# A hybrid attention and state-space layer: a third staging tile for weights, spaced norm tasks, deferred decay sums and early output tiles

## The chip, the cores and the metric

The kernel runs on one core of a Trainium2 chip. The metric is the device time of one execution in microseconds, as a median of runs. Smaller is better.

## What is computed

One layer on 2048 tokens of width 1024, in float32. With `hn` the RMSNorm of the tokens `h`, the reference does, cut short:

```python
proj = hn @ w_in[layer]
q, k, v, g_attn, z, xbc, dt_raw, q_mem, g_mem = jnp.split(proj, splits, axis=-1)
att = window_attention(rotary(q), rotary(k), v, attn_sink[layer]) * jax.nn.silu(g_attn)   # window of 128 to both sides
xs, bm, cm = jnp.split(jax.nn.silu(centred_depthwise_conv(xbc, conv_w[layer], conv_b[layer])), ...)
dt = jax.nn.softplus(dt_raw + dt_bias[layer])
y = ssd_scan(xs, dt[:, :, 0], a[0], bm, cm) + ssd_scan(backward) + d_skip[layer] * xs     # chunks of 128 tokens
ssd = gated_group_rmsnorm(y, z, ssd_norm_w[layer])
xat = softmax(q_mem . mk) @ mv * jax.nn.silu(g_mem)                                       # 256 memory tokens
h = h + jnp.concatenate([att, ssd, xat], axis=-1) @ w_out[layer]
return rms_norm(h, norm_out_w)
```

Attention has 16 query heads on 4 key heads of 64, the scan 8 heads of 64 in 2 groups with a state of 128, the memory attention 4 heads of 128.

## The kernel before

Large products are made exact enough by splitting each float32 operand into a rounded high part and a low part (`split`, L193 to L196: a cast on ScalarE, a difference on VectorE) and adding three matmuls (`split3`, L183). `mm` (L171) issues every matmul and `tr` (L179) every transpose, so nearly all of TensorE's work bears the lines L177 and L181.

The tokens go in four chunks of 512, the last first (loop near the end of `layer`, c = 3 to 0). A chunk's normalised and split tokens (xh, xl, 8 tiles each) stay in memory; the weights are streamed. `load_w` (L198) loads 128x1024 weights into a staging tile ws (two of them), and splits them into wh and wl (three each). Per chunk come the keys (`keys`, with the rotation `rope`), the values and step sizes (`values`, `steps`), and then four rounds g: query heads (`heads`), convolution (`conv`), gates (`z_gate`) and memory projection (`mem_project`). Attention, memory attention and the scan inside blocks of 128 tokens run as tasks between these products: `attention`, `mem_attention`, `ssd_local`. `ssd_local` needs for each block and group the decay sums that `ssd_load` (L600) makes from a loaded tile fb: four additions on ScalarE (L610), four on VectorE (L611) and an exponential (L612).

The next chunk's norms are made on the way. `cols_x` and `rstd_cols` (L294 to L306) run at once before round 1: for each of 4 or 5 blocks of tokens two half rows of x are loaded into a tile cu (three) and squared on ScalarE with a sum (L302). `rows_x` spreads the results over the partitions, and `norm_x` (L342) runs at once in round 2: eight tiles of x in transposed form are loaded into xp (four), multiplied on VectorE (L349) and stored. At the chunk's end `prep_x` loads them again into xp and splits them into xh and xl. The first keys' rotation borrows xp tiles as well.

After the last chunk the pools of the projections (`xhl`, `misc`) are closed and the output product begins. `mixed` (L983) loads and splits the mixed rows of a block of 128 tokens (mxl, mxh), `load_wo` (L965) the output weights through ws and xr tiles, `early` (L1004) adds the attention and memory half of a block, `out_block` (L1023) the rest and the final norm. The forward scan across blocks runs as tasks meanwhile: `incoming` (L743) makes what the states bring into a block, `carry` (L589) takes the state on, and `forward` (L774) adds it, gates it, sums squares (L790, L792) and normalises, one block at a time.

What sets the order: TensorE's order is written out by the program. A planner clock, `clock[0]`, is moved by `mm` and `tr` with a fixed cost for each; a task gives way with `yield t` and is taken up again when the planner's clock has gone on by t us (`tick`). `slot` and `reads` do the same for banks of the accumulator memory. `limits` says how many tasks of a kind run at once. The order on the other engines, and of the DMAs on SyncE's queue, is laid by the framework's scheduler at compile time, by a simulated timeline and by priorities (`tc.high_priority` moves instructions ahead), and each engine then runs its own list in that order. `tc.keep_in_program_order` puts an instruction behind the one written before it for the same engine.

## Time and profile before

| | |
|---|---|
| median of three runs | 1847.41 us (1845.33 to 1850.26) |
| the profiled execution | 1848.8 us |
| its span, first to last instruction | 1847.1 us |
| TensorE busy | 1755.7 us, 95% of the span |
| VectorE, ScalarE, GpSimd busy | 1179.9, 921.4, 260.3 us |
| mean granted TensorE clock | 0.985 of full speed |
| DMA | 347.59 MB, 188 GB/s in the mean |

The span is divided among chunks c = 3 to 0 up to about 1390 us, the change to the output product, and the output product with the forward scan from about 1495 to the end. A wait of TensorE stands in a row of the timeline in square brackets, with the instruction that ended it.

### The profile page before, as it was taken

What the parts mean: (1) busy time and instruction counts of PE and PEld (TensorE: products, weight loads), DVE (VectorE), ACT (ScalarE), POOL (GpSimd) and SP (SyncE); (2) the same over time, 40 slices, a digit from 0 to 9 for tenths busy, and PEclk for the clock granted to TensorE, in tenths of its full rate; (3) what the DMA queues carried; (4) which work ended last, traced back from release to release, by engine and by line L of the source; (5) the groups of instructions that cost most, each with busy time, mean ns of one, the idle gap of its engine ahead of it and who ended that gap; (6) DMA issues with size and microseconds to landing.
All of it is one profiled execution on the core that took longest, in us unless ns stands there. A gap on an engine that the chain in (4) does not pass through costs nothing. (4 is left out here: it accounts for less than half of the span.)

```text
span 1847.1 us, 26627 instructions
## 1 busy us (share of the span) xinstructions
PE 1755.7 (95%) x9242; PEld 1426.0 (77%) x9242; DVE 1179.9 (64%) x2681; ACT 921.4 (50%) x1985; POOL 260.3 (14%) x253
## 2 busy tenths in 40 slices
PE   7889999999799999999999989999998999999998
PEld 6878878877578787777778877778776777787886
DVE  7466666688576667778666777977677543443443
ACT  6237645664665566657555654656566411111121
POOL 1000000012200000121000002210111133333321
PEclk9989999999899999999999989999998999999999
DMA  7666364578653854776475466673658586566553
GB/s 237 211 197 187 123 214 146 152 241 244 210 169 122 268 165 150 240 245 206 142 211 161 133 205 195 190 214 118 197 179 265 165 251 182 164 180 180 171 176 120
DMA packets 264422, 347.59 MB, mean 188 GB/s; under 512 B 29536, under 2 KB 172000, under 8 KB 264288
## 3 DMA queue, kind: packets, MB, share of 16 engines
q1 hardware_dynamic: 264288, 345.90, 61.1%
q8 instruction: 73, 1.20, 0.3%
q14 instruction: 61, 0.50, 0.1%
HBM read 254.34 MB, written 91.49 MB: 187 GB/s over the span
## 5 line engine op out<-in xcount | busy, mean ns | idle before, releaser
L177 PE MATMUL pj<-xh,wh 128*128 128x512 f32 (+2 forms) x1296 | 506.6, 391 | 2.8 <-ACT xh L195 1.0
L177 PE MATMUL pj<-xl,wh 128*128 128x512 f32 (+2 forms) x1296 | 494.0, 381 | 4.8 <-DVE xl L196 4.8
L177 PE MATMUL pj<-xh,wl 128*128 128x512 f32 (+2 forms) x1296 | 494.7, 382 | 0.9 <-DVE wl L196 0.8
L196 DVE TENSOR_TENSOR wl<-ws,wh 128x1024 fp32r<-128x1024 f32 (+2 forms) x175 | 212.3, 1214 | 117.3 <-ACT wh L195 112.9
L177 PEld LDWEIGHTS pj<-xh,wl 128*128 128x128 f32 x1296 | 246.0, 190 | 46.9 <-DVE wl L196 2.7
L177 PEld LDWEIGHTS pj<-xh,wh 128*128 128x128 f32 x1296 | 246.7, 190 | 41.9 <-issue 3.7
L177 PEld LDWEIGHTS pj<-xl,wh 128*128 128x128 f32 x1296 | 246.8, 190 | 40.7 <-DVE xl L196 5.9
L195 ACT CAST wh<-ws 128x1024 fp32r<-128x1024 f32 (+2 forms) x175 | 180.0, 1029 | 179.3 <-PE pj L177 127.6
L546 DVE CUSTOM_DVE_ANT_0 pm<-s,band,sink 128x384 f32<-128x384 f32 (+1 forms) x256 | 150.3, 595 | 48.3 <-PE s L177 46.4
L554 ACT ACTIVATE pm<-pm,mx 128x385 f32<-128x385 f32 (+1 forms) x256 | 151.2, 595 | 55.5 <-DVE mx L552 55.5
L177 PE MATMUL pj<-woh,mxh 128*128 128x512 f32 x416 | 169.1, 407 | 0.0
L177 PE MATMUL pj<-woh,mxl 128*128 128x512 f32 x416 | 164.2, 395 | 0.0
L177 PE MATMUL pj<-wol,mxh 128*128 128x512 f32 x416 | 164.1, 394 | 0.0
L648 POOL TENSOR_TENSOR b<-nat,win 128x256 f32<-128x256 f32 x64 | 43.3, 697 | 841.2 <-ACT nat L632 841.2
L558 ACT ACTIVATE pm<-pm,den 128x384 f32<-128x384 f32 (+1 forms) x256 | 133.5, 595 | 6.9 <-DVE den L556 6.8
L572 ACT COPY pt<-t 128x512 f32<-128x512 f32 x120 | 69.4, 583 | 103.6 <-PE t L181 103.3
L195 ACT CAST mxh<-mxl 128x512 fp32r<-128x512 f32 x64 | 39.5, 617 | 162.8 <-DMA mxl<-mix_d 105.7
L181 PE MATMUL t<-ident,pm 128*128 128x128 f32 x736 | 103.8, 276 | 11.6 <-ACT nat L632 6.7
L181 PEld LDWEIGHTS t<-ident,pm 128*128 128x128 f32 x736 | 86.5, 142 | 34.6 <-ACT nat L632 7.6
L177 PE MATMUL s<-khh,qs 128*128 128x384 f32 (+1 forms) x256 | 94.7, 370 | 18.3 <-DVE mx L546 13.8
L484 DVE SCALAR_TENSOR_TENSOR cu<-raw,cw,cu 128x512 f32<-128x512 f32 (+2 forms) x128 | 99.3, 776 | 3.3 <-ACT cu L482 2.0
L177 PE MATMUL o<-pt,vg 128*64 128x256 f32 x736 | 93.8, 388 | 1.6 <-DVE dq L425 0.7
(222 smaller groups left out, 2842.8 us busy)
## 6 DMA issues: line engine op xcount, KB each, us to landing
ws<-in_w_in_dram SPq DMA_DIRECT2D x152, 512.0 KB, 4.2
q_d<-rt SPq DMA_DIRECT2D x32, 512.0 KB, 4.3
qs<-q_d SPq DMA_DIRECT2D x32, 512.0 KB, 6.1
fb<-f_d SPq DMA_DIRECT2D x32, 512.0 KB, 4.4
mxl<-mix_d SPq DMA_DIRECT2D x64, 256.0 KB, 4.1
mix_d<-ao SPq DMA_DIRECT2D x64, 128.0 KB, 3.5
xc<-xbc_d SPq DMA_DIRECT2D x32, 256.0 KB, 3.7
st_d<-carry SPq DMA_DIRECT2D x32, 256.0 KB, 3.9
```

What stands on the lines that cost most here:

```text
L177: nc.tensor.matmul(out, lhsT=lhsT, rhs=rhs, start=start, stop=stop)
L181: nc.tensor.transpose(out, in_, ident)
L195: nc.scalar.copy(hi, x)
L196: (eng or nc.vector).tensor_tensor(lo, x, as32(hi), ALU.subtract)
L484: nc.vector.scalar_tensor_tensor(u, raw[:, r0 + k:r0 + k + cnt], cw[:, i, k:k + 1], u, ALU.mult, ALU.add)
L546: nc.vector.tensor_tensor_reduce(pm[:, r, :w], ss[:, :w], band[:, ms], 1.0, sink8[:, 4 * g + r:4 * g + r + 1], ALU.add, ALU.max, mx[:, r:r ...
L554: nc.scalar.activation(pm[:, r, :w + 1], pm[:, r, :w + 1], AF.Exp, bias=mx[:, r:r + 1], scale=0.125, accum_out=den[:, r:r + 1])
L558: nc.scalar.activation(pm[:, r, :w], pm[:, r, :w], AF.Copy, scale=den[:, r:r + 1])
L572: nc.scalar.copy(pts[j], tt)
L648: nc.gpsimd.tensor_tensor(xd[:, d], nat[:, 0:256].rearrange("p (r e) -> p r e", r=4), win[:, d, 4 * g:4 * g + 4].unsqueeze(2).broadcast_to ...
```

## The change

- `load_w`'s staging tile ws gets three buffers; xp goes from four to three, and dt, fc, win from three to two.
- The squares for the next chunk's norms become a task of the new kind io, started at round 0: three loads go out, 8 us of planner time pass, then one square each 3 us, each followed by the next load. Their tiles are xp in place of cu. The squares are kept in program order. `diag_x` in round 2 waits for the task.
- `norm_x` becomes such a task, started in round 2; its multiplications are kept in program order and spaced by 2 us (5 more before the fourth and the seventh). `prep_x` waits for it.
- `ssd_load` gives back the loaded tile alone. A new `ssd_decay` makes the decay sums. For the first block and group it comes after the 12 us of planner time instead of before, and its first two instructions are kept in program order.
- `mem_attention` gives way for 4.5 instead of 3.0 us before its last product, `incoming` for 8.5 instead of 7.0, `forward` for 13 instead of 11.
- Two `forward` tasks run at once (yy in xc tiles, zz in b0 or b1 by turns), and all of them wait for `ssd_local`. The additions of `incoming` and the addition and gating of `forward` go from GpSimd to VectorE, and so do the state's two operations in `carry` for the forward direction.
- Before the projection pools are closed, block 15's first two mixed tiles are loaded and split in two ws tiles; `early` uses them for its first block. The planner then idles for 3 us. Of the next output weights rows 3 and 15 go through xr and row 13 through the tile nwo, instead of ws. `early` goes on until the third forward block is done instead of the second.

```diff
-    limits = {"att": 3, "mem": 1, "ssd": 1, "inc": 1, "fwd": 1}
+    limits = {"att": 3, "mem": 1, "ssd": 1, "inc": 1, "fwd": 2, "io": 1}
...
+    pin = tc.keep_in_program_order
...
-            ws = wsp.tile([P, D], F32, name="ws", bufs=2)
+            ws = wsp.tile([P, D], F32, name="ws", bufs=3)
...
-    def rstd_cols(src, nblk):
+    def cols_x(c, out):
...
+        def load():
+            if len(tiles) < len(jobs):
+                b, j = jobs[len(tiles)]
+                xn = misc.tile([P, XW], F32, name="xp", bufs=3)[:, :CH]
+                nc.sync.dma_start(xn, a["x"][s + b * P:s + (b + 1) * P, j * CH:(j + 1) * CH])
+                tiles.append(xn)
+
+        for _ in range(3):
+            load()
+        yield 8.0
+        for i, (b, j) in enumerate(jobs):
+            pin(nc.scalar.activation(tiles[i], tiles[i], AF.Square, accum_out=s2[:, j, b:b + 1]))
+            load()
+            yield 3.0
...
-    def norm_x(c, rb):
+    def norm_x(c, out):
...
+        for _ in range(3):
+            load()
+        yield 8.0
+        while "rows" not in out:
+            yield 1.0
         for kt in range(KT):
-            x32 = misc.tile([P, XW], F32, name="xp", bufs=4)[:, :w]
-            nc.sync.dma_start(x32, a["xT"][kt * P:(kt + 1) * P, s:s + w])
-            nc.vector.scalar_tensor_tensor(x32, x32, nw[:, kt:kt + 1], rb[:, :w], ALU.mult, ALU.mult)
-            nc.sync.dma_start(xn_d[kt, :, s:s + w], x32)
+            if kt in (3, 6):
+                yield 5.0
+            pin(nc.vector.scalar_tensor_tensor(tiles[kt], tiles[kt], nw[:, kt:kt + 1], out["rows"][:, :w],
+                                               ALU.mult, ALU.mult))
+            nc.sync.dma_start(xn_d[kt, :, s:s + w], tiles[kt])
+            load()
+            yield 2.0
...
+        eng = nc.gpsimd if d else nc.vector
+        eng.tensor_tensor(new.rearrange("p (r e) -> p r e", r=8), st.rearrange("p (r e) -> p r e", r=8), dec, ALU.mult)
+        eng.tensor_tensor(new, new, s, ALU.add)
...
+        return xc, fb
+
+    def ssd_decay(c, g, fb, first=False):
+        dt, fc, win = dts[c]
         ee = sp.tile([P, 4, P], F32, name="b0")
...
+            if r == 0 and first:
+                pin(i1)
+                pin(i2)
         nc.scalar.activation(ee, ee, AF.Exp)
...
-        nxt = ssd_load(*parts[0])
+        xc, fb = ssd_load(*parts[0])
         yield 12.0
+        nxt = xc, ssd_decay(*parts[0], fb, True)
...
-        nc.gpsimd.tensor_tensor(ef[:, 0], ef[:, 0], ef[:, 1], ALU.add)
+        nc.vector.tensor_tensor(ef[:, 0], ef[:, 0], ef[:, 1], ALU.add)
...
-        yy = sp.tile([P, 4, P], F32, name="b0")
+        yy = sp.tile([P, 4, P], F32, name="xc", bufs=2)
...
-        zz = sp.tile([P, 4, P], F32, name="b1")
+        zz = sp.tile([P, 4, P], F32, name=f"b{c % 2}")
...
-        nc.gpsimd.tensor_tensor(yy, yy, inc[c][:, 0], ALU.add)
+        nc.vector.tensor_tensor(yy, yy, inc[c][:, 0], ALU.add)
...
-            if c and g == 1:
-                cols = cols_x(c - 1)
+            if c and g == 0:
+                ahead = {}
+                cols_t = spawn("io", cols_x(c - 1, ahead))
             if c and g == 2:
-                dg = diag_x(c - 1, cols)
+                need(cols_t)
+                dg = diag_x(c - 1, ahead["cols"])
+                norm_t = spawn("io", norm_x(c - 1, ahead))
...
+    def mixed_tiles(c, qs, los, his):
+        mh, ml = {}, {}
+        for q, lo, hi in zip(qs, los, his):
+            nc.sync.dma_start(as32(lo), mix_d[4 * q:4 * q + 4, :, c * P:(c + 1) * P].rearrange("j p t -> p j t"))
+            split(hi, lo, as32(lo))
+            for j in range(4):
+                mh[4 * q + j], ml[4 * q + j] = hi[:, j], lo[:, j]
+        return mh, ml
+
+    first = [wsp.tile([P, D], F32R, name="ws", bufs=3).rearrange("p (u j t) -> p u j t", u=2, j=4) for _ in range(2)]
+    first = mixed_tiles(NB - 1, (0, 3), *([t[:, 0], t[:, 1]] for t in first))
     wx.close()
     fp = pool("fp")
     wo = pool("wo")
+    idle(clock[0] + 3.0)
...
-        ws = wsp.tile([P, D], F32, name="ws", bufs=2) if k % 2 else fp.tile([P, D], F32, name="xr", bufs=2)
+        ws = (wsp.tile([P, D], F32, name="ws", bufs=3) if k % 2 and pl is not wo else
+              fp.tile([P, D], F32, name="nwo") if k == 13 else fp.tile([P, D], F32, name="xr", bufs=2))
...
-        mh, ml = mixed(c, (0, 3))
+        mh, ml = mixed(c, (0, 3)) if begun else first
...
-    while last > 3 and not fwd[1].done:
+    while last > 3 and not fwd[2].done:
```

## Rows read from the trace of the kernel before

**Rows 1.** The page: the span, and busy time, share and count by engine

```profile
span 1847.1 us, 26627 instructions
PE 1755.7 (95%) x9242; PEld 1426.0 (77%) x9242; DVE 1179.9 (64%) x2681; ACT 921.4 (50%) x1985; POOL 260.3 (14%) x253
```

**Rows 2.** TensorE's timeline: start, length, instruction, [idle before and what ended it]

```profile
70.77 0.39 PE L177 MATMUL pj<-wl,xh 128*128 128x272 f32 x1 [3.06 <-DVE wl L196]
...
128.17 0.69 PE L177 MATMUL s<-khh,qs 128*128 128x384 f32 x1 [6.76 <-DVE mx L546]
...
469.11 0.69 PE L177 MATMUL s<-khh,qs 128*128 128x384 f32 x1 [3.82 <-ACT carry L670]
...
492.64 0.33 PE L181 MATMUL t<-ident,pm 128*128 128x128 f32 x1 [1.12 <-ACT pm L558]
...
499.15 0.48 PE L181 MATMUL t<-ident,pm 128*128 128x128 f32 x1 [4.72 <-ACT nat L632]
...
1095.31 0.49 PE L177 MATMUL o<-pt,mvt 128*128 128x512 f32 x1 [2.06 <-ACT pt L727]
...
1097.68 0.80 PE L177 MATMUL o<-mpm,mvt 128*128 128x512 f32 x1 [1.88 <-DVE mpm L731]
...
1403.38 0.79 PE L177 MATMUL pj<-wh,mxh 128*128 128x512 f32 x1 [8.86 <-ACT mxh L195]
```

**Rows 3.** Windows: stretch, length, PE busy (count), granted clock, DMA share, GB/s

```profile
123.80:134.04 10.24, 5.87 (x15) 0.50 0.36 100
468.55:471.96 3.41, 2.85 (x8) 0.50 0.63 207
495.86:502.68 6.82, 3.53 (x11) 0.50 0.56 162
...
1096.60:1103.43 6.83, 5.75 (x16) 0.50 0.89 265
1396.97:1407.21 10.24, 3.83 (x9) 0.50 1.00 336
```

**Rows 4.** ScalarE's timeline, the first decay sums

```profile
122.73 1.28 ACT L610 ACTIVATE b<-fb,fc 128x128 f32<-128x128 f32 x4 [6.24 <-DMA fb<-f_d]
```

**Rows 5.** Waits of ScalarE, 459 to 505: us in total, times, longest

```profile
ACT cu L302 <- DMA cu<-in_x_dram: 15.5, 5, 8.3
```

**Rows 6.** Waits of ScalarE, 1390 to 1425

```profile
ACT mxh L195 <- DMA mxl<-mix_d: 7.7, 1, 7.7
```

**Rows 7.** Windows, last stage: PE, PEld, DVE, ACT, POOL, clock, DMA share, GB/s

```profile
1495.00:1840.00 345.00, 335.37 (x1584) 275.58 (x1582) 142.78 (x300) 61.03 (x126) 109.44 (x100) 1.00 0.59 175
```

**Rows 8.** SyncE's timeline: the first weight loads into the new pool

```profile
1393.22 0.83 SPq L967 DMA_DIRECT2D xr<-in_w_out_dram  x2
```

**Rows 9.** Waits of TensorE, 1490 to 1845

```profile
PE t L177 <- DVE b L792: 8.1, 7, 2.0
PE t L177 <- DVE yo L804: 1.6, 3, 0.7
```

**Rows 10.** Instruction groups by form: count, busy us, mean ns, idle before

```profile
L789 POOL TENSOR_TENSOR b<-b,b 128x512 f32<-128x512 f32 x15 | 20.9, 1395 | 1.2
...
L196 DVE TENSOR_TENSOR mxl<-mxl,mxh 128x512 fp32r<-128x512 f32 x64 | 49.6, 776 | 71.0 <-ACT mxh L195 70.6
```

**Rows 11.** Waits for weights over the whole run, of TensorE and of ScalarE

```profile
PE pj L177 <- DVE wl L196: 3.9, 3, 3.1
...
ACT wh L195 <- DMA ws<-in_w_in_dram: 35.6, 13, 5.9
```

**Rows 12.** Who waited for xp's work; landing of the loads of L359

```profile
  PE pj L177: 5.8, 5
...
DMA to landing us min/median/max: 2.9/3.9/6.8
```

**Rows 13.** Waits of VectorE over the whole run

```profile
DVE xp L349 <- DMA xp<-in_xT_dram: 11.7, 4, 5.4
```

**Rows 14.** Waits of SyncE over the whole run

```profile
SPq L301 <- ACT cu L302: 27.3, 13, 4.7
```

More of the change, by code (lines that the diff above doesn't have):

```diff
@@ L236, in half @@
             if small:
-                return misc.tile([P, XW], F32, name="xp", bufs=4)[:, :2 * n].rearrange("p (j t) -> p j t", j=2)
+                return misc.tile([P, XW], F32, name="xp", bufs=3)[:, :2 * n].rearrange("p (j t) -> p j t", j=2)
             return misc.tile([P, 2, CH], F32, name=name)[:, :, :n]
@@ L292, in small_constants @@
         nc.vector.tensor_scalar(sink8, sink, 8.0, None, ALU.mult)
-    def rstd_cols(src, nblk):
+    def cols_x(c, out):
+        s, _ = window(c)
+        nblk = (CH * (c + 1) - s) // P
         ss = misc.tile([P, 8], F32, name="ss", bufs=2)
         s2 = misc.tile([P, 2, 8], F32, name="s2")
-        for b in range(nblk):
-            for j in range(2):
-                xn = misc.tile([P, XW], F32, name="cu", bufs=3)[:, :CH]
-                nc.sync.dma_start(xn, src[b * P:(b + 1) * P, j * CH:(j + 1) * CH])
-                nc.scalar.activation(xn, xn, AF.Square, accum_out=s2[:, j, b:b + 1])
+        jobs = [(b, j) for b in range(nblk) for j in range(2)]
+        tiles = []
+        def load():
[11 more added lines that the diff above has]
+            yield 3.0
         nc.vector.tensor_tensor(ss[:, :nblk], s2[:, 0, :nblk], s2[:, 1, :nblk], ALU.add)
@@ L305, in rstd_cols @@
         nc.gpsimd.tensor_tensor(ss[:, :nblk], ss[:, :nblk], neghalf[:, :nblk], ALU.pow)
-        return ss
+        out["cols"] = ss
     def diag(cols, n):
@@ L340, in rows_x, with load @@
         return rb
-    def norm_x(c, rb):
+    def norm_x(c, out):
         s, _ = window(c)
         w = CH * (c + 1) - s
-        for kt in range(KT):
-            x32 = misc.tile([P, XW], F32, name="xp", bufs=4)[:, :w]
-            nc.sync.dma_start(x32, a["xT"][kt * P:(kt + 1) * P, s:s + w])
-            nc.vector.scalar_tensor_tensor(x32, x32, nw[:, kt:kt + 1], rb[:, :w], ALU.mult, ALU.mult)
-            nc.sync.dma_start(xn_d[kt, :, s:s + w], x32)
+        tiles = []
+        def load():
+            if len(tiles) < KT:
+                x32 = misc.tile([P, XW], F32, name="xp", bufs=3)[:, :w]
+                nc.sync.dma_start(x32, a["xT"][len(tiles) * P:(len(tiles) + 1) * P, s:s + w])
+                tiles.append(x32)
+        for _ in range(3):
[3 more added lines that the diff above has]
+            yield 1.0
+        for kt in range(KT):
+            if kt in (3, 6):
[5 more added lines that the diff above has]
+            yield 2.0
     def prep_x(c, rb=None, raw=None):
@@ L356, in prep_x @@
         for kt in range(KT):
-            x32 = misc.tile([P, XW], F32, name="xp", bufs=4)[:, :w]
+            x32 = misc.tile([P, XW], F32, name="xp", bufs=3)[:, :w]
             if raw is None:
@@ L410, in steps @@
         yield 1.0
-        dt, fc, win = (sp.tile([P, 5, 2, 8], F32, name=nm, bufs=3)[:, :nb] for nm in ("dt", "fc", "win"))
+        dt, fc, win = (sp.tile([P, 5, 2, 8], F32, name=nm, bufs=2)[:, :nb] for nm in ("dt", "fc", "win"))
         for b in range(nb):
@@ L774, in forward @@
     def forward(c):
+        while not ssd_t.done:
+            yield 1.0
         if c == 0:
-            while not ssd_t.done:
-                yield 1.0
             spawn("inc", incoming(0))
         tl = slice(c * P, (c + 1) * P)
-        yy = sp.tile([P, 4, P], F32, name="b0")
+        yy = sp.tile([P, 4, P], F32, name="xc", bufs=2)
         nc.sync.dma_start(yy, y_d[:, :, tl].rearrange("j p t -> p j t"))
-        zz = sp.tile([P, 4, P], F32, name="b1")
+        zz = sp.tile([P, 4, P], F32, name=f"b{c % 2}")
         nc.sync.dma_start(zz, z_d[:, :, tl].rearrange("j p t -> p j t"))
@@ L938, in layer @@
             if c and g == 2:
-                norm_x(c - 1, rows_x(c - 1, dg))
+                ahead["rows"] = rows_x(c - 1, dg)
             for i in range(2 * g, 2 * g + 2) if c else ((0, 1, 2, 3, 4), (5, 6, 7), (), ())[g]:
@@ L952, in layer @@
         if c:
+            need(norm_t)
             with tc.high_priority(offset=200):
@@ L983, in mixed @@
     def mixed(c, qs):
-        mh, ml = {}, {}
-        for q in qs:
-            lo = fp.tile([P, 4, P], F32R, name="mxl", bufs=6)
-            nc.sync.dma_start(as32(lo), mix_d[4 * q:4 * q + 4, :, c * P:(c + 1) * P].rearrange("j p t -> p j t"))
-            hi = fp.tile([P, 4, P], F32R, name="mxh", bufs=5)
-            split(hi, lo, as32(lo))
-            for j in range(4):
-                mh[4 * q + j], ml[4 * q + j] = hi[:, j], lo[:, j]
-        return mh, ml
+        los, his = ([fp.tile([P, 4, P], F32R, name=nm, bufs=n) for _ in qs] for nm, n in (("mxl", 6), ("mxh", 5)))
+        return mixed_tiles(c, qs, los, his)
     def products(pf, mh, ml, order, first, last):
```

26 lines of the change are left out of this document (10 added, 16 removed).

## The prediction

> **What bounds the kernel now.** I read the page first. TensorE (PE) is busy 1755.7 us of a span of 1847.1 [rows 1]; the change removes no matmul, so what can be won is the 91.4 us in which PE idles and what the clock costs after an idle stretch. Next I went through PE's timeline for its longest idle stretches [rows 2]. Away from the first and last microseconds few of them are long: 6.76 us at 121 us, 3.82 at 465, two of 1.12 and one of 4.72 between 491 and 499, 2.06 and 1.88 at 1093 to 1098, 8.86 at 1395. Third, the windows: near each of these the granted clock is 0.50, which is 1.2 GHz instead of 2.4 [rows 3]. Work done at half clock takes twice as long, so half of PE's busy time there is lost. The reader is to see that a hole costs its length and a tail of 1.4 to 2.9 us behind it.
>
> Then, for each hole, what the engine that released PE had itself waited for. At 122.73 ScalarE began the decay sums of the scan's first block (L610) after 6.24 us of waiting for the DMA that fills fb [rows 4]. These sums are written in the program at the end of the chunk; the scheduler took them forward to a place where their load had not landed, and all of ScalarE's later work stood behind them. Between 459 and 505 ScalarE waited 15.5 us in five pieces, 8.3 the longest, for the x tiles whose squares (L302) make the next chunk's norms [rows 5]. At 1395 it waited 7.7 us for the first tile of mixed rows, whose memory comes free only when the projection pools are closed [rows 6]. So three groups of holes have one shape: an instruction sits in an in-order engine ahead of its data.
>
> **The change, part by part.** Profiled times are used throughout; the profiled execution took 1848.8 us (span 1847.1), the median of the runs 1847.4, so 1.4 us come off at the end.
>
> (A) *Squares as spaced tasks.* The 28 squares stay, 0.8 us each with their read, but three loads go out first, 8 us of planner time pass, then one square per 3 us, pinned in program order. Each later load has three squares' time, about 9 us, to land. What is removed: 3.82 + 1.12 + 1.12 + 4.72 = 10.8 us of holes [rows 2] and, at half clock, (2.85 + 3.53)/2 = 3.2 us [rows 3]: 14.0. The holes at 491 to 499 are ScalarE's backlog from the same waits, so they go along. I take nine tenths, 12.6. The other two passes over x (at 131 and 811 us) stalled ScalarE little, so I count nothing there.
>
> (B) *First decay sums deferred.* Load and sums are split, 12 us of planner time lie between, and the first pair is pinned. Removed: 6.76 + 5.87/2 = 9.7 us [rows 2, 3]. What is late next at that place is a weight cast that had waited for its load just before; I take 8.7.
>
> (C) *First output tiles early.* The two tiles for block 15 now use two of the three weight staging tiles, which don't wait for the pools to close, so their 7.7 us wait disappears. The hole and its tail are 8.86 + 3.83/2 = 10.8 us [rows 2, 3]. It doesn't close fully: three of the eight weight rows are ready; with 6 matmuls each at 0.21 us (the mean of the last stage: 335.37 us for 1584 [rows 7]) they feed PE for 3.8 us. The fourth row, and with it 13 and 15, moves from the staging tiles to tiles that open with the new pool, whose first loads were issued at 1393.2 [rows 8]. With a landing as slow as the 7.7 us seen there, and some 2 us of split, it is ready near 1403, which leaves some 5 us to wait; with 4 us of landing, about 1. The planner's idle of 3 us puts ready tasks in between and covers part. I take 7.0 (bounds 4 and 10.8, the whole).
>
> (D) *Scan sums on VectorE, two forward blocks at once, longer allowances.* In the last stage PE waits 8.1 us for the block's sum of squares and 1.6 for its diagonal [rows 9]: 9.7. The chain ahead has three GpSimd adds or products of about 1.39 us; a VectorE operation of the same 128x512 form on tiles in SBUF takes 0.78 [rows 10]. That shortens it by 1.8 us, the allowances grow by 1.5 and 2 us, and the next block's loads get buffers of their own. VectorE takes on 3 x 16 + 2 x 15 such operations, 61 us, in a stage of 345 us in which it is busy for 142.8 [rows 7]. The longest single wait is 2.0 us, so most go; the diagonal still waits for GpSimd's power. I take 6.5 (bounds 3 and 9.7).
>
> (E) *Memory attention's allowance, 3.0 to 4.5.* The holes at 1093 to 1098 are 2.06 + 1.88 and 5.75/2 = 2.9 of clock, 6.8 us [rows 2, 3]. 1.5 us more work placed before the first matmul takes 1.5 from them and perhaps half of the clock's part: 2.5 (bounds 0 and 6.8).
>
> (F) *Third weight staging tile.* PE waits for the low half of a weight only 3.9 us in all, 3.1 of it once at the start; ScalarE waits 35.6 us for weight loads, in 13 pieces, with other work behind [rows 11]. Most of that is hidden by PE's queued work. Bounds 0.8 and 8; I take 2.0, near the first row.
>
> Gains: 12.6 + 8.7 + 7.0 + 6.5 + 2.5 + 2.0 = 39.3 us.
>
> The costs. *xp from 4 tiles to 3.* At each of three chunk changes eight x tiles go through xp. Four loads were in flight ahead of PE's last use of the old chunk; now three. A late tile costs at worst one more load, 3.9 us median, and about 1.4 us of split: 5.3 us, 16 for three; at best nothing, as the splits also wait for PE to let go of the old tiles. Today PE waits 5.8 us in 5 pieces for work on xp [rows 12], nearer to the low end; I take 1.5 each, 4.5. The same tiles serve the first keys' rotation, where PE already waits 3.06 us at 70.8 [rows 2]; one more wait for a store, between 0 and 3.9 us; I take 1.5. *Norms pinned and spaced.* VectorE waits 11.7 us for their loads today, in 4 pieces [rows 13]; spacing takes that away, pinning behind the row sums can add as much. PE would feel a part; between 3 us gained and 3 lost, I take 0. *Start.* A third weight load can now go ahead of the memory tokens; with the DMA engines full they move 336 GB/s [rows 3], so its 512 KB put the first matmul off by 1.6 us (0 to 3.2). *What the holes hid.* With PE earlier, ScalarE and VectorE have less slack; 2.0. The earlier product tiles and x loads are the same DMAs on the same queue, only moved. Costs: 4.5 + 1.5 + 0 + 1.6 + 2.0 = 9.6.
>
> Here a rule of the Trainium skill speaks against the change. Today's waits on xp are small and uneven, 5.8 us in 5 pieces [rows 12]. The page "Perfetto Trace Analysis", section "Identifying Performance Opportunities", says that the same gap coming back on the engine that should be saturated can mean that too few buffers or too little room are left for the next tile. By that rule taking a tile away would bring one gap at each chunk change; the trace of before agrees only weakly, and what it would do here is the second rival, worked out from rows.
>
> Net 39.3 - 9.6 = 29.7: 1848.8 - 29.7 - 1.4 = 1817.7, say **1818 us**.
>
> **The rivals.**
> - *Nearly all closes.* Nine tenths of A to E (51.0 x 0.9 = 45.9), 3 for the weights, costs of 3: 1848.8 - 1.4 - 45.9 = 1801.5. For it: each hole has one plain cause. Against: C keeps its fourth weight row.
> - *Too few xp tiles.* Each chunk change pays the full extra round: 5.3 us and 1.4 of clock, as behind the 3.82 us hole [rows 2, 3], 6.7 x 3 = 20.1 in place of 4.5: 1818 + 15.6 = 1834. For it: the loads now go out one by one behind the splits. Against: splits wait for PE anyway.
> - *The holes wander.* The order on all engines but PE comes from a scheduler that took fb and x for landed when they were not [rows 4, 5]. The pins hold only named instructions; other loads can take the place. If half of the 39.3 comes back elsewhere: 1818 + 19.7 = 1838. This is also the case that the change doesn't do what it says.
> - *Slower: SyncE stands behind xp.* Each square's and norm's load beyond the first three waits for a tile: 7 + 7 + 5 squares and 3 x 5 norms, 34 loads. Today the like wait holds SyncE 27.3 us in 13 pieces, 2.1 each [rows 14]; 34 x 2.1 = 71 us, with weight loads queued behind. If half reaches PE the time is 1818 + 36 = 1854. It decides once the hold is longer than a weight's lead, about 5 us of PE work for one weight tile (24 matmuls). Against: three staging tiles give more lead than two, and the present holds hurt PE little.
>
> **How the numbers follow.** Forecast 0.52, nearly all 0.10, xp 0.16, wandering 0.16, slower 0.06. The range 1800 to 1842 takes in the first four cases and most of the bounds; the ends at which every term is best or worst at once are left out. A measurement of this kernel can tell about 0.3% (5.5 us) from no change. Below 1841.9 lie the forecast, the better case, nine tenths of the xp case and six tenths of the wandering: 0.52 + 0.10 + 0.14 + 0.10 = 0.86; above 1852.9 the last: 0.06; 0.08 between.
>
> **What would show it.** A and B: no ScalarE wait for the square's load or for fb of over 1 us, and PE without a hole of over 2 us at 121 and at 460 to 500, clock at 1.00 there. C: the first output matmul no longer waits for the mixed tile, and a wait of 0 to 4 us before the fourth weight row. D: PE's waits in the last stage under 3 us together. xp: waits for xl at the chunk changes of under 2 us each; 5 or more would give the rival. The prediction is wrong if a new hole of over 5 us opens elsewhere, or if SyncE's holds come ahead of weight loads that PE waits for.

## The result, and the profile after

The changed kernel takes 1830.15 us in the median of four runs (1823.8 to 1837.34); the kernel before took 1848.84 us beside it (1845.33 to 1850.3, four runs, the three of the table above among them). The ratio is 0.9896, with a 95% interval from 0.9872 to 0.992: 18.7 us faster, where 30 were forecast. All comparisons below are such ratios to the kernel before on the same chip, where it took about 1853 us in the median: a thousandth is 1.9 us.

The page of the changed kernel, against [rows 1]. Its profiled execution took 1832.96 us.

```profile
span 1831.3 us, 26618 instructions
PE 1756.1 (96%) x9242; PEld 1427.9 (78%) x9242; DVE 1224.0 (67%) x2759; ACT 921.1 (50%) x1985; POOL 162.8 (9%) x175
```

The span is 15.8 us shorter at the same number of matmuls. From all records of TensorE I added up, stage by stage, its idle time and half of its busy time in stretches at half clock: what a perfect cover would save. The stages are named by what stands in them. Beside before and after stand three of the experiments below.

```
us lost to idle + half clock          before  after   e9     e8     e11   forecast of the change
start, to 106                          24.5   20.9   23.7   25.9   21.9   cost 1.5 + 1.6, gain part of F
first decay sums (the hole at 121)     12.3    6.8    3.2   10.4    7.7   B, -8.7
squares (the holes at 460 to 500)      17.4   11.3    2.8   11.5   11.4   A, -12.6
to 909                                  6.5    7.3    8.0   11.7    7.9   part of F and of xp's 4.5
memory attention, to 1249              17.3   16.1   16.0   12.4   14.1   E, -2.5; part of xp's 4.5
closing, to the first forward block    15.0   16.2   14.6   16.1   22.7   C, -7.0
forward blocks                          8.9   12.3    2.2   12.1   13.6   D, -6.5
rest                                    7.0    7.5    7.7    7.1    7.1
sum                                   108.8   98.4   78.2  107.1  106.3
```

The sum falls by 10.4 us: idle by 16.2, while the half clock costs 5.8 more. The other 5.4 us of the span are TensorE's own busy time at full clock (1738.3 to 1732.9), which is no hole, and which I did not trace further.

TensorE's timeline of the changed kernel, long idle stretches away from the ends: those that answer to [rows 2], and two more, ahead of 370.98 and of 1657.89.

```profile
119.85 0.69 PE L177 MATMUL s<-khh,qs 128*128 128x384 f32 x1 [2.95 <-DVE mx L574]
...
370.98 0.66 PE L181 MATMUL t<-ident,pm 128*128 128x128 f32 x4 [2.83 <-ACT pt L600]
...
449.93 0.41 PE L177 MATMUL s<-khh,qs 128*128 128x384 f32 x1 [1.85 <-DMA qs<-q_d]
...
1075.39 0.80 PE L177 MATMUL o<-pt,mvt 128*128 128x512 f32 x1 [3.01 <-ACT pt L764]
1077.94 0.79 PE L177 MATMUL o<-mpm,mvt 128*128 128x512 f32 x1 [1.75 <-DVE mpm L768]
...
1388.87 0.49 PE L177 MATMUL pj<-woh,ws 128*128 128x512 f32 x1 [3.16 <-ACT woh L198]
1390.13 0.79 PE L177 MATMUL pj<-wol,ws 128*128 128x512 f32 x1 [0.77 <-DVE wol L199]
...
1657.89 0.67 PE L177 MATMUL t<-yo,ones 128*128 128x256 f32 x2 [3.25 <-DVE yo L841]
```

Holes of 6.76 and 8.86 us have become ones of about 3; of the four between 465 and 499 us, 1.85 us ahead of 449.93 and two of 1.3 are left. The last line is new: before, no wait for the diagonal yo was over 0.7 us [rows 9]. The one ahead of 370.98 lasted 1.15 us before; no run here tells what made it longer. It stands in the squares' stretch of the table. The windows show what the short holes still cost, against [rows 3] and [rows 7] (length, busy us of PE, PEld, DVE, ACT, POOL, then the granted clock, DMA share, GB/s).

```profile
119.48:126.31 6.83, 6.13 (x15) 4.70 (x16) 6.19 (x14) 2.28 (x4) 0.00 (x0) 0.50 0.40 109
1375.59:1382.42 6.83, 6.63 (x20) 4.61 (x21) 3.90 (x16) 1.45 (x3) 0.00 (x0) 0.50 1.06 345
1389.24:1396.07 6.83, 6.07 (x18) 3.60 (x18) 5.18 (x8) 2.54 (x4) 0.00 (x0) 0.50 0.64 221
1495.00:1840.00 345.00, 318.17 (x1487) 260.48 (x1485) 162.41 (x343) 58.26 (x123) 23.14 (x30) 0.98 0.56 159
```

A hole of 2.95 us at 117 is followed by 6.83 us at clock 0.50, of which TensorE was busy 6.13: the tail loses 3.07 us, as much as the 2.9 behind the hole of 6.76 before. Here the shorter hole did not have a shorter tail.

### The profile page after: what moved, and what is told of

It reads as the page before. It is cut to its first block, busy times and chain, and to the rows that moved or that the text cites. A ratio compares the mean times of both kernels' runs of the same rounds, so it can differ in the third digit from the quotient of the medians.

```text
span 1831.3 us, 26618 instructions
## 1 busy us (share of the span) xinstructions
PE 1756.1 (96%) x9242; PEld 1427.9 (78%) x9242; DVE 1224.0 (67%) x2759; ACT 921.1 (50%) x1985; POOL 162.8 (9%) x175
## 4 chain that ended last, share of the span: by engine, by line
PE 53%; DVE 7%; DMA 6%; ACT 5%; issue 2%; SPq 0%; POOL 0%; DVEq 0%; POOLq 0%; ACTq 0%
PE pj L177 38%; PE s L177 6%; PE o L177 5%; PE t L181 4%; ACT pm L582 2%; DMA mxl<-mix_d 1%; ACT pm L586 1%; DVE wl L199 1%; DMA xc<-y_d 1%; DVE pm L574 1%; DMA fb<-ef_d 1%; DMA mix_d<-xc 1%; ACT wh L198 1%; DVE cu L512 1%; PE t L177 1%
## 5 line engine op out<-in xcount | busy, mean ns | idle before, releaser
L177 PE MATMUL pj<-wol,mxh 128*128 128x512 f32 x406 | 160.4, 395 | 0.0
L199 DVE TENSOR_TENSOR mxl<-mxl,mxh 128x512 fp32r<-128x512 f32 x62 | 42.7, 690 | 86.8 <-ACT mxh L198 86.3
```

The lines of the kernel that those rows point to most:

```text
L177: nc.tensor.matmul(out, lhsT=lhsT, rhs=rhs, start=start, stop=stop)
L199: (eng or nc.vector).tensor_tensor(lo, x, as32(hi), ALU.subtract)
```

## The experiments

**e1, the addition of y back on GpSimd.** In the changed kernel's forward stage TensorE waits for the diagonal yo (waits from 1490 to 1845 us: us in total, times, longest),

```profile
PE t L177 <- DVE yo L841: 10.3, 6, 3.3
```

VectorE waits for the load of y (waits from 1450 on),

```profile
DVE xc L824 <- DMA xc<-y_d: 10.6, 6, 4.6
```

and SyncE, over the whole run, holds that load back until a store of mixed rows has landed.

```profile
SPq L819 <- DMA mix_d<-xc: 50.0, 14, 5.9
```

VectorE's timeline ahead of the hole that ends at 1657.89 shows how these hang together:

```profile
1649.15 0.69 DVE L199 TENSOR_TENSOR mxl<-mxl,mxh 128x512 fp32r<-128x512 f32 x1 [8.34 <-ACT mxh L198]
...
1654.52 0.15 DVE L837 TENSOR_SCALAR rn<-t 128x2 f32<-128x2 f32 x1
1655.93 0.69 DVE L824 TENSOR_TENSOR xc<-xc,fb 128x512 f32<-128x512 f32 x1 [1.26 <-DMA xc<-y_d]
1656.66 0.69 DVE L826 TENSOR_TENSOR xc<-xc,b 128x512 f32<-128x512 f32 x1
1657.27 0.47 DVE L841 TENSOR_SCALAR yo<-ident,rn 128x128 f32<-128x128 f32 x2
```

The diagonal at 1657.27, for which TensorE stands, needs nothing of the two operations ahead of it: they belong to the next block, and the first waits for a y whose tile came free only with an older block's store. VectorE runs its list in order, so TensorE waits for that load.

The load is not the whole of the wait. The scaling factor rn, which the diagonal does need, was itself late (1654.52): it stands behind operations that VectorE began only at 1649.15, after 8.34 us of waiting for a cast on ScalarE. I paired each of TensorE's six waits with VectorE's wait for y ahead of the same diagonal and took the shorter of the two: the loads of y can account for 5.4 of the 10.3 us at most. Ahead of the wait that ended at 1535.41, 1.08 us long, VectorE did not wait for y at all: between rn and the diagonal stood only the two operations themselves.

```diff
-        nc.vector.tensor_tensor(yy, yy, inc[c][:, 0], ALU.add)
+        nc.gpsimd.tensor_tensor(yy, yy, inc[c][:, 0], ALU.add)
```

> The changed kernel with one operation put back: forward's addition of the incoming part to y (L824) runs on GpSimd again, everything else as changed. Theory: that addition waits for the load of y, and on VectorE the diagonal of the block before stands behind it. Then VectorE's 10.6 us of waits for that load go to GpSimd, TensorE's waits for the diagonal in the last stage fall from 10.3 us to under 3, and the time falls by 6 to 9 us against the changed kernel, to about 1823. Rival: the diagonal is late because two blocks at once crowd VectorE; then the waits stay near 10 us and the time at about 1830.

Measured: 1825.42 us, ratio 0.9846 (0.9824 to 0.9868), 9.3 us better than the change. TensorE's waits in the same stretch of e1,

```profile
PE t L177 <- DVE yo L841: 2.4, 2, 2.2
```

and GpSimd's from 1450 on:

```profile
POOL xc L824 <- DMA xc<-y_d: 32.8, 3, 14.9
```

GpSimd stands 32.8 us for the same loads. VectorE still stands for what comes of them, at the product behind the addition (waits of VectorE from 1450 on),

```profile
DVE xc L826 <- POOL xc L824: 19.5, 8, 6.0
```

and the longest of these stands ahead of the longer of the two waits for the diagonal that e1 has left, 2.17 us (VectorE's timeline in e1):

```profile
1667.35 0.69 DVE L826 TENSOR_TENSOR xc<-xc,b 128x512 f32<-128x512 f32 x1 [6.02 <-POOL xc L824]
```

So the engine of this one operation is worth 9.3 us, as the theory had it, and the rival fell: with two blocks still at once, the waits for the diagonal went. That the wait for the load made all of the 9.3 us is not shown: VectorE's list is another one around the edit too (its waits for ScalarE's casts of the mixed tiles fell from 81.2 to 56.2 us in this stretch). The addition kept on VectorE, but behind the diagonal, would tell; no run has it. And e1 has a new hole of 3.81 us, at the first forward block's sum of squares.

**e2, all four first decay sums pinned.** The pin of the change holds only the first pair (r = 0). In the changed kernel the other three sums run on ScalarE at 117.03 us, some 240 us early; ScalarE's timeline there, with a square ahead of them:

```profile
112.67 0.63 ACT L317 ACTIVATE xp<-xp 128x512 f32<-128x512 f32 x1 [5.46 <-DMA xp<-in_x_dram]
...
117.03 0.98 ACT L642 ACTIVATE b<-fb,fc 128x128 f32<-128x128 f32 x3 [0.94 <-DMA fb<-f_d]
```

```diff
-            if r == 0 and first:
+            if first:
```

> The changed kernel with all eight of the first block's decay sums kept in program order instead of the first of four on each engine. Theory: the other three float forward to 117 us but cost only the 0.94 us that ScalarE waits there; the hole of 2.95 us and its tail of 3.1 come from ScalarE's 5.5 us wait for a square's load just before. Then all four sums move to about 360 us, ScalarE no longer waits for fb at 117, and the hole stays at 2 to 4 us; time within 2 us of the changed kernel, 1828 to 1832. Rival: the sums that still float are what is left of the hole; then it goes, with 6 us of time, to about 1824.

Measured: 1832.07 us, ratio 0.9886 (0.9866 to 0.9907), no difference. All sums now run near 358; the square still stands 5.41 us for its load, and the hole at 117 stays at 2.48 us.

**e3, the squares further apart.**

```diff
-            yield 3.0
+            yield 5.0
```

> The changed kernel with 5 instead of 3 us of planner time between the squares of the next chunk's norms. Theory: three squares' time (9 us) is too short for a load that is issued late on SyncE's queue and takes 4 to 10 us to land; ScalarE's waits for these loads, 26.3 us in 6 pieces, fall under 8, the hole at 117 us and most of the 3.8 us between 448 and 483 go, and the time falls by 5 to 9 us to about 1823. Rival: the waits are hidden anyway and the holes have other causes; then the waits fall and the time stays at 1830.

Measured: 1826.04 us, ratio 0.9853 (0.9831 to 0.9876), 8.0 us better by the medians, though the intervals touch. ScalarE's waits for the squares' loads over the whole run, in the change:

```profile
ACT xp L317 <- DMA xp<-in_x_dram: 26.3, 6, 7.4
```

in e3:

```profile
ACT xp L317 <- DMA xp<-in_x_dram: 11.9, 3, 4.8
```

and ScalarE's timeline in e3 at 111 us:

```profile
111.64 0.63 ACT L317 ACTIVATE xp<-xp 128x512 f32<-128x512 f32 x1 [4.80 <-DMA xp<-in_x_dram]
```

Between 448 and 500 the loss is largely gone, but at 111 the wait stays. In the changed kernel the squares ahead of that wait started at 104.47, 105.56 and 106.48 us: one microsecond apart, where the planner had put 3. The planner's clock spaces them in the program; on ScalarE they run as soon as their data is there, and three that were held up run together. Their loads then go out together, at 105.20 and 106.52 on SyncE, and take 6.8 us to land (median there).

**e4, the weight casts ahead of the mixed tiles' casts.**

```diff
+            if woh_ins:
+                with tc.issue_after(woh_ins[13]):
+                    split(hi, lo, as32(lo))
+            else:
+                split(hi, lo, as32(lo))
...
-        split(woh[k], wol[k], ws, nc.vector)
+        nc.scalar.copy(woh[k], ws)
+        woh_ins[k] = [i for i in nc.cur_bb.bb.instructions if i.engine == mybir.EngineType.Activation][-1]
+        nc.vector.tensor_tensor(wol[k], ws, as32(woh[k]), ALU.subtract)
```

> The changed kernel with ScalarE's casts of later blocks' mixed tiles queued behind the casts of the first three output weight rows loaded into the new pool (rows 3, 12 and 13). Theory: row 3 has landed at 1378.0 but its cast stands at 1387.8 behind six casts that wait for mixed tiles; with the order turned, the cast starts by 1380, TensorE's waits of 3.16 and 0.77 us before row 3 go and with them most of the 3.0 us at half clock, so 5 to 7 us less, about 1824. Rival: the DMA engines are full there and the next rows or the mixed tiles become late by as much; then the hole only moves and the time stays at 1830.

Measured: 1832.05 us, ratio 0.9893 (0.9866 to 0.9919): nothing. My theory fell. With ScalarE free, the cast of row 3 comes 3.7 us earlier, but still only at 1384.09, where the theory had 1380 (ScalarE's timeline in e4):

```profile
1384.09 1.99 ACT L1029 CAST woh<-xr 128x1024 fp32r<-128x1024 f32 x2 [2.62 <-issue]
```

The rounded row takes memory from which the last gate's store, z_d, still reads; in e4's trace that store lands at 1384.02. In the changed kernel that store stands behind six loads of mixed tiles (SyncE's timeline),

```profile
1373.57 0.91 SPq L1021 DMA_DIRECT2D xr<-in_w_out_dram  x2
...
1375.00 6.39 SPq L1005 DMA_DIRECT2D mxl<-mix_d  x6
1381.49 0.78 SPq L522 DMA_DIRECT2D z_d<-gm  x1
```

and the cast comes after it (ScalarE's timeline):

```profile
1387.78 1.99 ACT L198 CAST woh<-xr 128x1024 fp32r<-128x1024 f32 x2
```

**e5, that store ahead of the loads.**

```diff
+        z_store[0] = [v for v in nc.cur_bb.bb.instructions if v.engine == mybir.EngineType.SP][-1]
...
-        return mixed_tiles(c, qs, los, his)
+        with tc.issue_after(z_store[0]):
+            return mixed_tiles(c, qs, los, his)
```

> The changed kernel with one order turned round on SyncE: the six loads of mixed tiles that hold the last block's values stand behind the last gate's store, not ahead of it. Theory (the closing's fourth weight row can't be cast before that store has landed, since its rounded form takes the memory from which the store reads): the store is issued near 1377 us and lands near 1382, where it was 1381.49 and 1386.84; the cast of row 3 starts by 1383, where it was 1387.78; the holes of 3.16 and 0.77 us at 1385 to 1390 come under 1 us in sum and the 3.0 us at half clock behind them lessen; the time falls by 4 to 6 us. Rival (the store takes its time because the DMA engines are full, whatever its place): it lands within 1.5 us of where it did, the holes stay and the time with them.

Measured: 1826.26 us, ratio 0.9858 (0.9827 to 0.9889), 7.0 us better by the medians, though the intervals touch. The first line of `+` stands in `z_gate`, behind its store. In e5 the store goes out at 1374.39 instead of 1381.49, and ScalarE's timeline has

```profile
1380.83 2.00 ACT L198 CAST woh<-xr 128x1024 fp32r<-128x1024 f32 x2 [1.20 <-DMA z_d<-gm]
```

while TensorE's has

```profile
1383.19 0.51 PE L177 MATMUL pj<-wol,ws 128*128 128x512 f32 x1 [0.76 <-DVE wol L199]
...
1392.75 0.50 PE L177 MATMUL pj<-wol,ws 128*128 128x512 f32 x1 [1.37 <-DVE wol L199]
```

The cast comes 6.95 us earlier and now names the store as what it waited for. The hole of 3.16 is gone; 0.76 and 1.37 us remain, more than the 1 us expected, and the closing falls from 16.2 to 9.0 us lost.

**e6, no squares; e10, no squares and all first decay sums pinned.** In both the loads and squares of the later tokens' norms are left out and a constant stands for their sum.

```diff
-            pin(nc.scalar.activation(tiles[i], tiles[i], AF.Square, accum_out=s2[:, j, b:b + 1]))
-            load()
...
+        nc.vector.memset(s2, 512.0)
```

> The changed kernel without the 28 loads of x and the 28 squares on ScalarE for the later tokens' norms; a constant stands in their sum's place, so this part of the computation is left out. Theory (what is left of the holes at 117 us and from 448 to 483 us is ScalarE standing at squares whose loads haven't landed): the hole of 2.95 us at 117 and its 3.07 us at half clock go, as do most of the 3.8 us of holes and 1.7 us of clock from 448 to 483; with what ScalarE no longer does the time falls by 8 to 12 us. Rival (the holes are made by the later tokens' q, which comes back late from DRAM, and by the maximum on VectorE, squares or not): the holes stay within 1 us of their size and the time falls by under 4 us.

> The changed kernel without the later tokens' x loads and squares (a constant stands in their sum's place, so that part of the computation is left out) and with all four first decay sums pinned to their place. Without the squares alone, ScalarE stood 6.29 us at 115.90 us for the load of the first decay sum that isn't pinned, and the hole at 116 us grew to 5.01 us; with the pins alone it stood 5.41 us at a square, and the hole stayed at 2.48. Theory (two waits of ScalarE lie over one another there, and either alone makes the hole): with both gone the hole is under 1 us, its half clock gone, and the time 4 to 8 us under that without the squares alone, a ratio of 0.981 to 0.983. Rival (a third thing, such as the order of the maximum on VectorE, makes it): a hole of over 2 us stays at 114 to 120 us.

Measured: e6 1827.3 us, ratio 0.9853 (0.9821 to 0.9885); e10 1816.84 us, 0.9801 (0.9781 to 0.9821). Without the squares the stretch from 448 to 485 us has hardly a hole (TensorE busy 36.32 of 37 us), but the one at 116 grew to 5.01 us: ScalarE's timeline in e6 has

```profile
115.90 0.98 ACT L638 ACTIVATE b<-fb,fc 128x128 f32<-128x128 f32 x3 [6.29 <-DMA fb<-f_d]
```

With the pins as well, the window from 115 to 126 us in e10 is full of TensorE's work at full clock.

```profile
115.00:126.00 11.00, 11.00 (x57) 9.82 (x57) 10.25 (x25) 4.87 (x7) 0.00 (x0) 1.00 0.56 175
```

So two waits of ScalarE lay over one another at this place, a square's and that of the unpinned sums, and either alone makes the hole. That is why e2 alone gave nothing. By the medians the pins are worth some 9.6 us once the squares are out of the way, more than the 4 to 8 expected; the intervals touch.

**e7, more room in the memory attention.**

```diff
-        yield 4.5
+        yield 8.0
```

> The changed kernel with the allowance of the memory attention's step raised from 4.5 to 8.0 us, so that the list puts more matmuls between its steps. Theory (the two holes at 1072 and 1076 us are TensorE waiting for ScalarE's exponentials and the mean, with too little put between): the holes of 3.01 and 1.75 us and the 2.45 us at half clock there go, and the time falls by 5 to 7 us. Rival (the steps' distance isn't set by the allowance, as from 3.0 to 4.5, which left the loss there at 7.2 us after 6.8): the loss there stays over 4 us and the time within 3 us.

Measured: 1850.54 us, ratio 0.999 (0.9969 to 1.0011), 17 us worse than the change. The window where the two holes were is nearly full of TensorE's work in e7, so the holes do go;

```profile
1068.00:1082.00 14.00, 13.28 (x99) 12.14 (x98) 11.82 (x38) 9.30 (x27) 1.14 (x1) 1.00 0.63 209
```

but the later work moved, and other holes opened, the longest in the closing (TensorE's timeline):

```profile
1404.79 0.79 PE L177 MATMUL pj<-woh,ws 128*128 128x512 f32 x1 [8.95 <-ACT woh L198]
```

The theory was right on the two holes and wrong on the time; the rival was wrong on both. An allowance shifts the whole list behind it; by which steps it came to 8.95 us I did not follow.

**e8, both buffer edits undone; e11, the third weight tile alone undone.** The first pair of lines is in both (at all three places of ws), the second in e8 alone (at all four of xp).

```diff
-            ws = wsp.tile([P, D], F32, name="ws", bufs=3)
+            ws = wsp.tile([P, D], F32, name="ws", bufs=2)
...
-                xn = misc.tile([P, XW], F32, name="xp", bufs=3)[:, :CH]
+                xn = misc.tile([P, XW], F32, name="xp", bufs=4)[:, :CH]
```

> The changed kernel with the buffers as they were before: two staging tiles for weights and four for rows of x, where the change has three and three. The forecast's terms (third weight tile worth 2.0 us, fewer x tiles costing 4.5, the first keys' rotation 1.5) say that undoing the swap gives 2 to 4 us back: waits of TensorE for the low part of x go from 6.6 us in 8 to under 5 in 4, the waits for weight loads rise by under 3 us. Rival one (the fourth x tile is what the squares' loads need): the squares' waits for loads fall from 26.3 to under 15 us and the time by 6 us or more. Rival two (the third weight tile carries the gain of the early rows): the time rises by 3 us or more.

> The changed kernel with two staging tiles for weights and three for rows of x: the third weight tile alone undone, the x tile not given back. With both undone the ratio was 0.9939, 8 us over the change. Theory (the third weight tile is worth those 8 us and the fourth x tile nothing): a ratio of 0.992 to 0.996, waits of TensorE at weights in the first 110 us as with both undone (idle before the first cumulative sum's store 20.98 us, where the change has 17.83). Rival (the fourth x tile gives back 3 to 6 us, as the forecast had it, and the third weight tile is worth more still): a ratio of 0.996 to 1.0.

Measured: e8 0.9939 (0.9916 to 0.9963), e11 0.9932 (0.9912 to 0.9953): 8.0 and 6.7 us worse than the change. Expected had been that undoing the swap gives back 2 to 4 us; rival two of e8 came in, and e11's theory. Waits over the whole run, of ScalarE for weight loads and of TensorE for the low part of x (before: 35.6 us in 13 for the first [rows 11]), in the change:

```profile
ACT wh L198 <- DMA ws<-in_w_in_dram: 7.6, 2, 5.5
...
PE pj L177 <- DVE xl L199: 6.6, 8, 2.4
```

in e8:

```profile
ACT wh L198 <- DMA ws<-in_w_in_dram: 35.9, 14, 4.6
...
PE pj L177 <- DVE xl L199: 4.1, 3, 1.6
```

and in e11:

```profile
ACT wh L198 <- DMA ws<-in_w_in_dram: 40.1, 14, 7.4
...
PE pj L177 <- DVE xl L199: 5.6, 6, 2.4
```

The third weight tile takes 28 to 33 us of waits from ScalarE, and 7 to 8 us of time. The fourth x tile (e8 against e11) changes TensorE's wait for x by 1.5 us and the time by nothing that shows; that is with two weight tiles, and no run has it with three. Where the loss comes back differs: in e8 in the first 120 us and up to 909, in e11 in the closing (22.7 against 16.2). The loss of an extra tile is not at one place. In the closing of both runs the early mixed tiles take both staging tiles that there are, so e11's loss there may be theirs and not the streamed weights'; no run separates the two.

**e12, the first output tiles late again**, and the weight rows 3, 13 and 15 in staging tiles. The planner's idle of 3 us, also part of C, stays.

```diff
-    first = mixed_tiles(NB - 1, (0, 3), *([t[:, 0], t[:, 1]] for t in first))
...
-        mh, ml = mixed(c, (0, 3)) if begun else first
+        mh, ml = mixed(c, (0, 3))
```

> The changed kernel with the first output tiles as they were before: block 15's mixed tiles in the pool that opens when the projection pools close, weight rows 3, 13 and 15 in staging tiles again. Theory (term C gave nothing in net, because the wait for the mixed tile went over to the fourth weight row): the hole of 7 to 9 us with its tail comes back at the closing's first product, the holes of 3.16 and 0.77 us and their 3.0 us at half clock go, and the time stays within 3 us of the change, a ratio of 0.988 to 0.991. Rival one (the early tiles are worth their 7.0 us all the same, as forecast): a ratio of 0.992 to 0.995. Rival two (they cost more than they give): 0.987 or less.

Measured: 1831.43 us, ratio 0.9888 (0.9864 to 0.9913), the change's own. The closing's first product waits again, but only this long (TensorE's timeline in e12):

```profile
1379.02 0.80 PE L177 MATMUL pj<-wh,mxh 128*128 128x512 f32 x1 [3.42 <-ACT mxh L198]
```

I had expected 7 to 9 us. So of the 8.86 us that this hole measured before [rows 2] more than half goes without the early tiles. The planner's idle, which puts ready tasks there, may be what does it, or another part of the change; no run here takes the idle out.

**e9, four edits together** (e1, e2, e3 and e5).

> Four edits of the runs so far together: the addition of y back on GpSimd, all four first decay sums pinned, squares 5.0 us apart, the mixed loads behind the last gate's store. Alone they gave ratios to the kernel before of 0.9846, 0.9886, 0.9853 and 0.9858 where the change itself gave 0.9896. Theory (they sit at different places and each takes its own hole): the gains of 9.2, 1.8, 8.0 and 7.0 us add up to 26 us, the ratio comes to 0.973 to 0.979. Rival (a hole closed early only moves the work behind it against another engine): half of it at most, a ratio of 0.982 or over, with a new hole of over 3 us somewhere between 120 and 1370 us.

Measured: 1815.97 us (1810.88 to 1821.21), ratio 0.9792 (0.9765 to 0.9819): 19.3 us better than the change and 37 better than before, the fastest of the kernels that compute the whole. Of the sum of the single gains, 26 us, three quarters come; the interval reaches the edge of the theory's span, and one new hole of over 3 us has opened, though at the first forward block and not where the rival had it; e1 alone has it too (3.81 us). TensorE's timeline in e9:

```profile
1456.27 0.61 PE L177 MATMUL t<-ones,b 128*128 128x1 f32 x4 [3.41 <-DVE b L832]
```

The table above shows where it gains on the change: squares 8.5, forward blocks 10.1, first decay sums 3.6 us; the start lost 2.8.

## Why the prediction was right, and where it was not

The direction and the range held: 1830 lies between 1800 and 1842. The forecast of 1818 missed 12 us. Gain terms of 39.3 us were set against costs of 9.6; neither came as put, and that the sum still fell into the range is in part luck: D came 9.9 us short, C 7.0 and A 6.5, while F gave 5 to 6 more than taken and xp's cost of 4.5 did not show. Of the prediction's own signs, C's came (3.16 us before the fourth row, where 0 to 4 were given). A's and B's did not (a square waited 5.46 us for its load, a hole of 2.95 us and the half clock stayed), nor did D's (10.3 us of waits for the diagonal, where under 3 were asked).

- **D failed, with the wrong sign** (6.5 us gained in the sum, 3.4 us lost in the table). The step was "That shortens it by 1.8 us": the durations were right, in fact better (0.69 us for each of these operations on VectorE, where 0.78 was taken). But it counted the operations' own time alone, and left out where the addition of y would stand in VectorE's list, ahead of the diagonal, and that it waits for a DMA. On GpSimd the additions of y had stood a long time for their loads; the waits of GpSimd in the kernel before, 1450 to 1845 us, have the row that I should have read:

```profile
POOL b L787 <- DMA b<-y_d: 99.8, 13, 11.6
```

The bound "3 to 9.7" left out a loss, though no row excluded one. With this one addition back on GpSimd (e1, added up as in the table) the forward blocks lose 2.4 us, 6.5 less than before; but the closing ahead of them, with e1's new hole, loses 21.4 where the change loses 16.2. The other parts of D were not undone alone. The page "GPSIMD Engine Reference" of the Trainium skill, section "Engine selection", sends elementwise additions on tiles to VectorE, since GpSimd takes about twice as long. This case's durations agree (0.69 us against 1.29 in e1), and e1 shows the time going the other way by 9.3 us: on the engine with the faster addition it stands ahead of the diagonal for which TensorE waits.

- **C's early tiles gave nothing that shows** (7.0 taken; e12 is 1.5 us from the change, within the intervals; the planner's idle was not tested). The step that failed: "The fourth row is ready near 1403 ... with 4 us of landing, about 1". The mechanism, the fourth row coming late, was right; its price was not made by the load. The rows' loads went out at 1373.57, and still the cast came at 1387.78, because of a store that stood behind the six new loads on SyncE. I had written "the same DMAs on the same queue, only moved" and costed that at nothing; what they were moved past was the point. With the store first (e5) the closing loses 9.0 us in place of 15.0 before: 6.0 of the 7.0. Beside it, 1.74 us of hole and 3.3 of clock at 1374 stand in the changed closing, for which the sum had no term.

- **A had the right cause and half its size** (6.1 of 12.6 between 361 and 552 us). The step that failed is "three squares' time, about 9 us, to land": it took the planner's spacing for ScalarE's, and left out that a load can go out late. Between 420 and 446 us the loads took 5.0 to 9.7 us to land, and the first of them went out only at 420.00, over 6 us after the square at 413.17 whose tile it took. So the waits for these loads did not go: over the whole run they rose from 19.9 us to 26.3, and in this pass over x they are 13.6 us after 15.5 [rows 5], some 40 us earlier in the run. TensorE's holes shrank all the same. "The holes at 491 to 499 are ScalarE's backlog" held: two of 1.3 us are left, which e6, without squares, doesn't have. e3 gave 8.0 us more. And the first pass over x, for which A counted nothing, now has the wait of 5.46 us at 112.

- **B had the right cause** (5.6 of 8.7). What stayed is not the weight cast that I named as next, but a square, brought there by A, and three of the four sums that the pin doesn't hold. I read "the first pair is pinned" and did not ask about the other three. e10 shows both.

- **E gave nothing**: 3.01 + 1.75 us of holes and 2.45 of clock are 7.2 us after 6.8 before. The bound from below held; e7 shows that room enough closes the holes and what it costs elsewhere.

- **F and the costs of xp were mis-sized, in opposite ways.** F was taken as 2.0, "near the first row", that is TensorE's own 3.9 us of waits. e8 and e11 put it at 7 to 8, near the upper bound. ScalarE's 35.6 us [rows 11] were the row to go by: TensorE may feel them under other names, since a late cast holds up the exponentials and copies queued behind it; that is how I read it, no row shows it. xp cost 4.5 in the forecast; waits for xl went from 4.8 us in 4 pieces to 6.6 in 8, the longest 2.4, and e8 against e11 shows no price, with two weight tiles. The rule of the Trainium skill ("Perfetto Trace Analysis", "Identifying Performance Opportunities": one gap that keeps coming back can mean too few buffers) did not decide here: there are twice as many gaps, but small ones. The rival built on it, 1834, lies nearest to the measured time by accident, as its cause did not come.

- **The norms** at 0 held: VectorE's waits for their loads fell from 11.7 us [rows 13] to 1.5 in 2; no run shows what that gave. **The start** was to cost 1.6 and lost 3.6 us less than before. **The slower rival** did not come: SyncE was held 7.9 us in 6 pieces for the squares' loads, where it had been 27.3 in 13 [rows 14], and 35.8 in 13 and 8.0 in 6 for the norms' loads, and the time fell.

- **Wandering holes**, the rival with 0.16 at 1838, describe best what happened. Of the 39.3 us of gains some 16 came (A 6.1, B 5.6, F 7 to 8, less D's 3.4), and the places of the rest have names: the diagonal (D), the gate's store (C), the square at 112 (A, B). As far as the runs show they did not wander by chance; at each stood an instruction, or a DMA, that the change had moved.

## What to carry to other kernels

Before an operation is given to a faster engine, look up what it waited for where it was: if that is a DMA, the wait moves too, and on an engine that runs its list in order it holds up all that stands behind. Look up as well what it will stand ahead of there. Before a load is moved forward, write down each queue entry that it passes, stores above all, and who needs the memory that those stores release. And size a buffer by the waits of the engine that uses it, also where TensorE's own waits for it look small, as here they told more; then test each edit alone, as here one of six cost 9 us inside a kernel that was faster in the whole.

## What was not expected of the hardware

A hole need not be long for the half clock to follow it. In the changed kernel a hole of 1.74 us at 1374.05 us, after one of 0.34, stands ahead of the 6.83 us at 0.50 from 1375.59 on, which cost 3.3 us, more than the hole. After one of 1.46 us at 911 the window reads 1.00:

```profile
905.00:918.00 13.00, 11.54 (x65) 9.03 (x65) 10.75 (x29) 9.15 (x26) 0.00 (x0) 1.00 0.21 56
```

The kernel before lost 17.4 us to the half clock in eight stretches, the changed one, with less idle time, 23.2 in ten. So the clock's part did not go down with the holes' length here. It went where the hole itself went: e9 lost 13.9 us, e10's window at 115 none.

A load can be slow without a high rate. From 100 to 116 us of the changed kernel the DMA view has (busy share in tenths, then GB/s, slice by slice)

```profile
DMA  9971017898999989899999999899999982189889
GB/s 440 399 307 21 10 51 184 282 287 210 236 241 210 225 164 389 343 256 138 164 210 215 210 210 241 276 399 374 371 369 407 405 333 77 56 302 343 220 241 241
```

The four loads for squares that went out in it took 6.8 us in the median, with the engines busy at eight or nine tenths and the rate mostly between 140 and 260 GB/s, where the closing had 345 in the windows above. What filled the engines at so low a rate, no run here tells.
